# High halves of weights and feed-forward activations on ScalarE instead of GpSimd, in a two-layer hybrid mixer network

## The chip, the cores and the metric

The kernel runs on one core of a Trainium2 chip. Times are device microseconds (us) of one execution. Engines are named TensorE (PE in the profile; PEld are its weight loads), VectorE (DVE), ScalarE (ACT), GpSimd (POOL) and SyncE (SP, which only issues DMAs here). Each engine works through its own list of instructions in order; an instruction that waits holds up all that stand behind it on that engine.

## The reference, cut to what matters

A backbone of two layers runs over 256 context tokens and 256 latent tokens, 1024 wide. Each layer is a half-step gated feed-forward, four token mixers in parallel on one normalised input, and a second half-step feed-forward; all are modulated by shift, scale and gate vectors made from a conditioning vector.

```
def swiglu(h, w_up, w_down):
    a, g = jnp.split(h @ w_up, 2, axis=-1)
    return (jax.nn.silu(a) * g) @ w_down
...
def pre_norm(t, gain, m, i):
    return modulate(rms_norm(t, gain), m[..., 3 * i, :], m[..., 3 * i + 1, :])
```

The mixers are a gated delta rule, a long convolution (Hyena, by Fourier transforms), a state-space scan and a gated linear attention. Their inputs come from one projection `w_in`, their outputs go through `w_branch` and sigmoid gates into `w_out`. In the last layer only the latent tokens are needed behind the scans. All is float32.

## The kernel before, in words

**Products in three matmuls.** A float32 product is made of three matmuls in a faster, rounded format (float32r). Each operand x is split into a high half (x rounded to that format) and a low half (x minus the high half); the result is high·high + low·high + high·low. For activations the halves are called `hh`/`hl` (normalised input), `ah`/`al` (feed-forward hidden values), `yh`/`yl` (mixer outputs) and `mh`/`ml` (merged mixers). For weights they are `wh` and `wl`.

**Weights in chunks.** `wchunk` loads a chunk of 512 x 256 weights (512 KB, a tile of 128 x 1024) by a DMA from SyncE into `raw`, makes `wh` from it and then `wl` = `raw` − `wh`. There are three buffers each for `raw`, `wh` and `wl`, so a chunk's `wh` can be made once TensorE has left the chunk three before it. `dense_T_g` then issues, for each of two output tiles and four row blocks, the three matmuls of 512 columns (256 in most of layer 1 behind its mixers' start); `dense_tok_g` does the same with the weights as the moving side (lines 791 to 793).

**Feed-forward.** `ffn` goes through pairs of hidden tiles: two chunks give the `a` half, two the `g` half. ScalarE makes `sil` = silu(a) from PSUM (line 682), VectorE multiplies it by g in PSUM (line 687), then `split` makes `ah` and VectorE `al` (line 260). In the first three feed-forward stages VectorE also works through the modulation sums `aa` (lines 528 and 530), a fixed number for every two chunks: `aa` = `aw`·c + `aa` over loaded pieces of `w_ada`.

**Norms.** Before a stage, ScalarE makes `hh` (line 657), GpSimd the unrounded value `v` (line 658) and VectorE `hl` = `v` − `hh` (line 659).

**Mixers.** Two generators are woven together: the chain (gated delta rule, scans, convolutions; short steps on all engines) and the dense projections. A table of numbers sets how far each runs ahead. The engines' lists are then made by a scheduler that takes instructions by priority and its own estimate of when each is ready; `wchunk` gives its halves a higher priority than their place (`high_priority`, 240 places), except for the very first chunk.

**Who makes high halves.** Line 248: GpSimd makes `wh` and VectorE `wl` (line 249). In layer 0's mixers (`n_wp0` = 5) every fifth chunk has `wh` on ScalarE (line 245) and `wl` on GpSimd (line 246). `ah` is made by GpSimd (`i_acts` = 1, line 257), `yh` too, `mh` by ScalarE (line 255). The first feed-forward projection's first chunks have their own code (line 367), as do the few narrow columns at the start of the mixers (line 809): GpSimd.

Of the kernel before, what the change touches and what calls it, by code (L numbers as in the profile page):

```python
# [8 lines left out]
F32 = mybir.dt.float32  # L9
F32R = mybir.dt.float32r  # L10
I32 = mybir.dt.int32
AF = mybir.ActivationFunctionType
ALU = mybir.AluOpType
# [87 lines left out]
def const_inputs():  # L101
# [24 lines left out]
         "i_Td": 1, "i_W": 1, "i_bd": 0, "i_bm": 1, "i_ce": 1, "i_cz": 1, "i_gr": 1, "i_hy": 1, "i_scr": 1, "slack":  # L126
# [5 lines left out]

# [4 lines left out]
class Kern:  # L137
# [93 lines left out]
    def wchunk(self, src, nk, ncol):  # L231

        nc = self.nc
        n = nk * ncol
        r = self.raw(src.rearrange("(k p) c -> p k c", p=128), (128, nk, ncol))
        hi = self.pw.tile([128, 1024], F32R, name=self.nm("wh"), tag="wh", bufs=3)
        lo = self.pw.tile([128, 1024], F32R, name=self.nm("wl"), tag="wl", bufs=3)
        h = hi[:, :n].rearrange("p (a b) -> p a b", a=nk)
        l = lo[:, :n].rearrange("p (a b) -> p a b", a=nk)
        hold = self.nw < self.gen('n_hold', 2)  # L240
        with self.tc.issue_after(self.gate.ins) if hold else self.tc.high_priority(offset=self.gen('n_hp', 250)):
            self.nw += 1
            e = self.gen(f"n_wp{self.part}", 0)
            if e and self.nw % e == 0:
                nc.scalar.activation(h, r, AF.Copy)
                nc.gpsimd.tensor_tensor(l, r, h.bitcast(F32), op=ALU.subtract)
            else:
                nc.gpsimd.tensor_scalar(h, r, 1.0, 1.0, op0=ALU.mult, op1=ALU.mult)  # L248
                nc.vector.tensor_tensor(l, r, h.bitcast(F32), op=ALU.subtract)  # L249
        return h, l  # L250

    def split(self, x, hi, lo, eng="act"):
# [1813 lines left out]
```

## Time and profile before

| | |
|---|---|
| median of 3 runs | 2844.51 us (2844.41 to 2846.63) |
| profiled execution | 2847.14 us, its span 2845.2 us |
| granted TensorE clock, mean | 0.978 of full speed |
| busy: TensorE / its weight loads | 2689.9 us (95%) / 2289.9 us (80%) |
| busy: VectorE | 2036.7 us (72%), 3763 instructions |
| busy: GpSimd | 1038.9 us (37%), 1007 instructions |
| busy: ScalarE | 529.4 us (19%), 1044 instructions |
| DMA | 382.66 MB, 134 GB/s over the span |

The span is the time from the first to the last instruction of the profiled execution; the execution's own time has a little around it. Matmuls overlap in the records: one of 512 columns is listed with about 0.37 us, while the next starts 0.23 us later, so it is the idle time of TensorE and the granted clock that show what is lost, not the sum of the durations. A wait is put down to the instruction that ended last of those waited for.

Stages on the time axis, from the lines that run in them: start and first chunks to 71 us; first feed-forward of layer 0 to 450; mixers of layer 0 and their output projection to 1285; second feed-forward to 1690; first feed-forward of layer 1 to 2070; mixers of layer 1 to 2640; last feed-forward and output to the end.

### The profile page before, as it was taken

To read this page: it belongs to the slowest core of one execution; us is meant where nothing else is said; L and a number is where in the kernel's file an instruction comes from. 1 tells how busy PE (TensorE), PEld (TensorE's weight loads), DVE (VectorE), ACT (ScalarE), POOL (GpSimd) and SP (SyncE) were. 2 spreads that over 40 slices of the span, in tenths; PEclk is the share of its full clock that TensorE was granted. 3 is DMA by queue.
4 is the path that set the end of the run, shared out by engine and by line. 5 is a ranking of instruction groups with operands and counts; after the bars stand their busy time and mean duration, and the time that the engine had idled before them with its cause. 6 is when DMAs were issued, how large, how long until landed. Compare 5 with 4: busy or idle time off the path is not lost. (4 is left out here: it accounts for less than half of the span.)

```text
span 2845.2 us, 40232 instructions
## 1 busy us (share of the span) xinstructions
PE 2689.9 (95%) x15131; PEld 2289.9 (80%) x15131; DVE 2036.7 (72%) x3763; ACT 529.4 (19%) x1044; POOL 1038.9 (37%) x1007
## 2 busy tenths in 40 slices
PE   7999999989999999999999999999987899989998
PEld 5777767778888878877778877788877798889998
DVE  5999875699575564459965469966479877778656
ACT  2000012533224231111000020000042322311100
POOL 4333313221332554535322233322244233455443
PEclk8999999999999999999999999999999999999999
DMA  9556534322434233234644336543333344445554
GB/s 273 168 178 198 174 109 132 89 75 71 141 112 131 77 100 101 85 116 145 180 145 130 102 110 181 176 146 117 95 89 108 96 138 133 143 150 186 154 185 142
DMA packets 369697, 382.66 MB, mean 134 GB/s; under 512 B 43466, under 2 KB 317544, under 8 KB 369504
## 3 DMA queue, kind: packets, MB, share of 16 engines
q1 hardware_dynamic: 347568, 363.67, 42.7%
q10 hardware_dynamic: 21936, 16.44, 1.8%
q8 instruction: 119, 1.95, 0.3%
q14 instruction: 74, 0.61, 0.1%
HBM read 355.79 MB, written 24.25 MB: 134 GB/s over the span
## 5 line engine op out<-in xcount | busy, mean ns | idle before, releaser
L248 POOL TENSOR_SCALAR wh<-raw 128x1024 fp32r<-128x1024 f32 (+1 forms) x460 | 570.7, 1241 | 1181.7 <-PE pmm L296 716.5
L294 PE MATMUL pmm<-hh,wh 128*128 128x512 f32 (+1 forms) x2432 | 887.0, 365 | 14.8 <-ACT raw L964 8.7
L295 PE MATMUL pmm<-hh,wl 128*128 128x512 f32 (+1 forms) x2432 | 880.7, 362 | 18.8 <-DVE wl L249 18.8
L296 PE MATMUL pmm<-hl,wh 128*128 128x512 f32 (+1 forms) x2432 | 878.8, 362 | 6.3 <-DVE hl L659 6.3
L249 DVE TENSOR_TENSOR wl<-raw,wh 128x1024 fp32r<-128x1024 f32 (+1 forms) x460 | 581.8, 1266 | 388.4 <-POOL wh L248 387.7
L295 PEld LDWEIGHTS pmm<-hh,wl 128*128 128x128 f32 x2432 | 467.6, 192 | 91.1 <-DVE wl L249 26.1
L294 PEld LDWEIGHTS pmm<-hh,wh 128*128 128x128 f32 x2432 | 467.5, 192 | 86.7 <-issue 15.4
L296 PEld LDWEIGHTS pmm<-hl,wh 128*128 128x128 f32 x2432 | 467.0, 192 | 76.2 <-DVE hl L659 10.6
L530 DVE SCALAR_TENSOR_TENSOR aa<-aw,cond,aa 128x256 f32<-128x256 f32 x896 | 423.9, 534 | 0.5 <-DMA aw<-in_w_ada 0.5
L295 PE MATMUL pmm<-ah,wl 128*128 128x512 f32 (+1 forms) x704 | 256.6, 364 | 1.6 <-DVE wl L249 1.4
L294 PE MATMUL pmm<-ah,wh 128*128 128x512 f32 (+1 forms) x704 | 258.0, 366 | 0.0
L296 PE MATMUL pmm<-al,wh 128*128 128x512 f32 (+1 forms) x704 | 256.5, 364 | 0.0
L682 ACT ACTIVATE sil<-pmm 128x512 f32<-128x512 f32 (+1 forms) x88 | 48.0, 545 | 812.2 <-PE pmm L296 773.3
L257 POOL TENSOR_SCALAR ah<-sil 128x512 fp32r<-128x512 f32 (+1 forms) x88 | 71.5, 813 | 251.5 <-DVE sil L687 228.8
L295 PEld LDWEIGHTS pmm<-ah,wl 128*128 128x128 f32 x704 | 133.2, 189 | 23.9 <-DVE wl L249 3.3
L294 PEld LDWEIGHTS pmm<-ah,wh 128*128 128x128 f32 x704 | 133.3, 189 | 23.2 <-issue 2.0
L296 PEld LDWEIGHTS pmm<-al,wh 128*128 128x128 f32 x704 | 133.3, 189 | 21.5 <-issue 0.8
L793 PE MATMUL pmm<-wl,hh 128*128 128x256 f32 x416 | 120.1, 289 | 6.3 <-DVE wl L249 6.3
L791 PE MATMUL pmm<-wh,hh 128*128 128x256 f32 x416 | 120.8, 290 | 0.0
L792 PE MATMUL pmm<-wh,hl 128*128 128x256 f32 x416 | 119.6, 288 | 0.0
L260 DVE TENSOR_TENSOR al<-sil,ah 128x512 fp32r<-128x512 f32 (+1 forms) x88 | 93.0, 1057 | 18.4 <-POOL ah L257 18.4
L296 PE MATMUL pmm<-yl,wh 128*128 128x512 f32 (+1 forms) x256 | 86.5, 338 | 1.3 <-DVE yl L260 1.3
(435 smaller groups left out, 3667.3 us busy)
## 6 DMA issues: line engine op xcount, KB each, us to landing
raw<-in_ffn_up SPq DMA_DIRECT2D x172, 512.0 KB
raw<-in_w_in SPq DMA_DIRECT2D x164, 512.0 KB
aw<-in_w_ada SPq DMA_DIRECT2D x288, 256.0 KB
raw<-in_ffn_down SPq DMA_DIRECT2D x80, 512.0 KB
raw<-in_w_branch SPq DMA_DIRECT2D x32, 512.0 KB
fe<-pk SPq DMA_DIRECT2D x42, 256.0 KB
raw<-in_w_out SPq DMA_DIRECT2D x16, 512.0 KB
pk<-pj ACTq DMA_DIRECT2D x26, 256.0 KB
```

The costliest lines, as they stand in the source:

```text
L248: nc.gpsimd.tensor_scalar(h, r, 1.0, 1.0, op0=ALU.mult, op1=ALU.mult)
L249: nc.vector.tensor_tensor(l, r, h.bitcast(F32), op=ALU.subtract)
L257: nc.gpsimd.tensor_scalar(hi, x, 1.0, 1.0, op0=ALU.mult, op1=ALU.mult)
L260: nc.vector.tensor_tensor(lo, x, hi.bitcast(F32), op=ALU.subtract)
L294: nc.tensor.matmul(o, h[:, k, js], rh[:, tj:t1], start=st, stop=False)
L295: nc.tensor.matmul(o, l[:, k, js], rh[:, tj:t1], start=False, stop=False)
L296: self.last_mm = nc.tensor.matmul(o, h[:, k, js], rl[:, tj:t1], start=False, stop=sp)
L530: nc.vector.scalar_tensor_tensor(a, x, c, a, op0=ALU.mult, op1=ALU.add)
L682: self.last_act = nc.scalar.activation(s[:, t0:t1], ps, AF.Silu)
L791: nc.tensor.matmul(o, rh[:, ts], h[:, k, :], start=st, stop=False, skip_group_check=True)
L792: nc.tensor.matmul(o, rl[:, ts], h[:, k, :], start=False, stop=False, skip_group_check=True)
L793: self.last_mm = nc.tensor.matmul(o, rh[:, ts], l[:, k, :], start=False, stop=sp, skip_group_check=True)
```

## The change

In `wchunk` every chunk now takes one path: ScalarE copies `raw` into `wh` (rounding it), VectorE subtracts. The choice by `n_wp0` is gone from the code, and with it the 20 low halves that GpSimd made. `i_acts` goes from 1 to 0, so ScalarE also makes `ah`. The own code of the first projection and the narrow columns stays with GpSimd, as do `v`, `yh` and the chain's steps. Behind `wchunk` the line numbers of the changed kernel are 5 lower than before.

```diff
-        {"i_acts": 1, "n_ga01": 3, ...
+        {"i_acts": 0, "n_ga01": 3, ...
...
-            e = self.gen(f"n_wp{self.part}", 0)
-            if e and self.nw % e == 0:
-                nc.scalar.activation(h, r, AF.Copy)
-                nc.gpsimd.tensor_tensor(l, r, h.bitcast(F32), op=ALU.subtract)
-            else:
-                nc.gpsimd.tensor_scalar(h, r, 1.0, 1.0, op0=ALU.mult, op1=ALU.mult)
-                nc.vector.tensor_tensor(l, r, h.bitcast(F32), op=ALU.subtract)
+            nc.scalar.activation(h, r, AF.Copy)
+            nc.vector.tensor_tensor(l, r, h.bitcast(F32), op=ALU.subtract)
```

The scheduler makes new lists of it. In the first feed-forward stage of layer 0, GpSimd's list before has the two kinds of high halves of one pair of hidden tiles between each other:

```order
L248 TENSOR_SCALAR wh_1129<-raw_1127 128x1024
L248 TENSOR_SCALAR wh_1161<-raw_1159 128x1024
L257 TENSOR_SCALAR ah_1076<-sil_985 128x512
L248 TENSOR_SCALAR wh_1218<-raw_1216 128x1024
L257 TENSOR_SCALAR ah_1093<-sil_999 128x512
L248 TENSOR_SCALAR wh_1270<-raw_1268 128x1024
```

In the changed kernel the same six stand on ScalarE, with the `sil` of the pair between them:

```order
L677 ACTIVATE sil_985<-pmm_929 128x512
L243 ACTIVATE wh_1129<-raw_1127 128x1024
L677 ACTIVATE sil_999<-pmm_942 128x512
L243 ACTIVATE wh_1161<-raw_1159 128x1024
L250 ACTIVATE ah_1076<-sil_985 128x512
L243 ACTIVATE wh_1218<-raw_1216 128x1024
L250 ACTIVATE ah_1093<-sil_999 128x512
L243 ACTIVATE wh_1270<-raw_1268 128x1024
```

The order of the six among themselves is kept; `sil` comes first for each of the two leading `wh`.

In layer 1's mixers, in the gated delta rule, ScalarE's list before holds chain steps alone (`qkv` are convolved inputs on their way through silu, `raw_18260` the projection out of PSUM, `pj` a projection for the convolution branch):

```order
L964 ACTIVATE raw_18260<-pmm_18197 128x512
L874 ACTIVATE qkv_18259<-raw_18260,vB_14423 128x512
L964 ACTIVATE raw_18281<-pmm_18210 128x512
L874 ACTIVATE qkv_18280<-raw_18281,vB_14423 128x512
L967 ACTIVATE qkv_18259<-qkv_18259 128x512
L967 ACTIVATE qkv_18280<-qkv_18280 128x512
L1267 ACTIVATE pj_18609<-pmm_18524 128x512
```

At that place in the changed kernel three `wh` stand among them, which GpSimd had in a row before:

```order
L959 ACTIVATE raw_18260<-pmm_18197 128x512
L869 ACTIVATE qkv_18259<-raw_18260,vB_14423 128x512
L959 ACTIVATE raw_18281<-pmm_18210 128x512
L869 ACTIVATE qkv_18280<-raw_18281,vB_14423 128x512
L243 ACTIVATE wh_18649<-raw_18647 128x1024
L962 ACTIVATE qkv_18259<-qkv_18259 128x512
L962 ACTIVATE qkv_18280<-qkv_18280 128x512
L243 ACTIVATE wh_18710<-raw_18708 128x1024
L243 ACTIVATE wh_18765<-raw_18763 128x1024
L1262 ACTIVATE pj_18609<-pmm_18524 128x512
```

Two of them stand behind the `qkv` of line 962, which waits for VectorE's convolution steps.

## Rows read from the trace of the kernel before

**Rows 1.** The page: busy us, share and instructions of each engine.

```profile
PE 2689.9 (95%) x15131; PEld 2289.9 (80%) x15131; DVE 2036.7 (72%) x3763; ACT 529.4 (19%) x1044; POOL 1038.9 (37%) x1007
```

**Rows 2.** Stretches, both mixers: start:end, length; busy us (count) by engine.

```profile
450.00:1285.00 835.00, 798.66 (x4383) 676.01 (x4382) 528.45 (x1024) 248.76 (x480) 324.96 (x326) 0.99 0.34 101
...
2070.00:2640.00 570.00, 509.15 (x3615) 468.06 (x3615) 452.75 (x865) 154.10 (x329) 240.51 (x260) 0.96 0.44 131
```

**Rows 3.** TensorE's waits: whole run (first three), 71:450, 1285:1690, 1690:2070 us.

```profile
PE pmm L295 <- DVE wl L249: 20.2, 18, 3.2
...
PE pmm L296 <- DVE hl L659: 6.3, 11, 1.5
...
PE pmm L793 <- DVE wl L249: 6.3, 2, 4.2
...
PE pmm L295 <- DVE wl L249: 7.0, 5, 3.2
...
PE pmm L295 <- DVE wl L249: 5.6, 5, 2.5
...
PE pmm L295 <- DVE wl L249: 6.1, 6, 1.6
```

**Rows 4.** A stretch of the first feed-forward: PE, PEld, DVE, ACT, POOL.

```profile
142.30:284.50 142.20, 137.59 (x617) 109.89 (x616) 141.15 (x277) 5.08 (x10) 47.67 (x30) 0.99 0.62 188
```

**Rows 5.** Order of time, 126:136 us, GpSimd and VectorE: start, us, instruction.

```profile
128.03 2.50 POOL L248 TENSOR_SCALAR wh<-raw 128x1024 fp32r<-128x1024 f32 x2
...
128.10 1.52 DVE L260 TENSOR_TENSOR al<-sil,ah 128x512 fp32r<-128x512 f32 x1 [0.51 <-POOL ah L257]
...
129.55 5.21 DVE L530 SCALAR_TENSOR_TENSOR aa<-aw,cond,aa 128x256 f32<-128x256 f32 x9
...
134.68 1.21 DVE L249 TENSOR_TENSOR wl<-raw,wh 128x1024 fp32r<-128x1024 f32 x1
```

**Rows 6.** A stretch behind a `wl` wait; the clock stands behind POOL's time.

```profile
137.40:140.70 3.30, 3.30 (x9) 2.52 (x9) 3.30 (x9) 0.00 (x0) 0.00 (x0) 0.50 0.40 117
```

**Rows 7.** Groups on GpSimd the change removes: busy us, mean ns | idle.

```profile
L248 POOL TENSOR_SCALAR wh<-raw 128x1024 fp32r<-128x1024 f32 x444 | 558.3, 1258 | 1137.6 <-PE pmm L296 682.2 <-issue 206.0 <-PE pmm L792 81.3
...
L248 POOL TENSOR_SCALAR wh<-raw 128x512 fp32r<-128x512 f32 x16 | 12.4, 774 | 44.1 <-PE pmm L296 34.3 <-DMA raw<-in_ffn_down 7.1 <-issue 2.7
...
L257 POOL TENSOR_SCALAR ah<-sil 128x512 fp32r<-128x512 f32 (+1 forms) x88 | 71.5, 813 | 251.5 <-DVE sil L687 228.8
...
L246 POOL TENSOR_TENSOR wl<-raw,wh 128x1024 fp32r<-128x1024 f32 x20 | 48.4, 2421 | 83.2 <-ACT wh L245 70.7 <-issue 7.1 <-DVE X L1067 5.4
```

**Rows 8.** Groups on ScalarE of the same kind that exist already.

```profile
L245 ACT ACTIVATE wh<-raw 128x1024 fp32r<-128x1024 f32 x20 | 21.2, 1058 | 58.7 <-PE pmm L296 49.9 <-PE pmm L792 5.1 <-DMA pk<-gqk 2.2
...
L255 ACT ACTIVATE mh<-x 128x512 fp32r<-128x512 f32 x8 | 5.1, 632 | 27.1 <-POOL x L1899 27.1
```

**Rows 9.** VectorE: `aa` min/median/max ns; then groups with their means.

```profile
L530 DVE SCALAR_TENSOR_TENSOR aa<-aw,cond,aa x896: 465/473/1336, 62.0 to 1949.5; 128x256 f32<-128x256 f32 x180
...
L530 DVE SCALAR_TENSOR_TENSOR aa<-aw,cond,aa 128x256 f32<-128x256 f32 x896 | 423.9, 534 | 0.5 <-DMA aw<-in_w_ada 0.5
...
L260 DVE TENSOR_TENSOR al<-sil,ah 128x512 fp32r<-128x512 f32 x66 | 75.0, 1137 | 18.2 <-POOL ah L257 18.2
...
L687 DVE TENSOR_TENSOR sil<-sil,pmm 128x512 f32<-128x512 f32 x66 | 44.8, 679 | 8.9 <-PE pmm L296 8.8
```

**Rows 10.** The chain that ended last, dense matmuls, 256 columns: start, us.

```profile
2657.20 0.12 PE pmm L294
```

**Rows 11.** ScalarE's waits, 2070 to 2640 us: us, times, longest.

```profile
ACT gt L1883 <- PE pmm L296: 59.7, 23, 9.2
...
ACT qkv L967 <- DVE qkv L887: 22.3, 5, 15.0
```

**Rows 12.** Order of time, layer 1's gated delta rule, VectorE and ScalarE.

```profile
2196.62 6.13 DVE L887 SCALAR_TENSOR_TENSOR qkv<-raw,vB,qkv 128x508 f32<-128x508 f32 x8
...
2202.13 1.35 ACT L967 ACTIVATE qkv<-qkv 128x512 f32<-128x512 f32 x2 [14.98 <-DVE qkv L887]
```

2 rows, old and new, of the table PACE are left out of this document.

## The prediction

> **What bounds the kernel now.** I read the engine totals first: TensorE is busy for 2689.9 of 2845.2 us, and no other engine comes near [rows 1]. So the change can only be worth what TensorE stands idle, 155 us, and what it runs at half clock. By stages (the table of stretches) the idle time sits in the two mixer stages, 835.0 − 798.7 = 36 us in layer 0 and 570.0 − 509.2 = 61 us in layer 1 [rows 2]; the rest lies in the start and in the feed-forward stages. Then I asked who ended TensorE's waits. In the three feed-forward stages that run beside the modulation sums it is above all one thing: a low half `wl` that VectorE has not yet made, 7.0 + 5.6 + 6.1 = 18.7 us in 16 of the 18 waits of this kind [rows 3]. In the mixers it is many short waits for the chain of recurrent steps; `wl` accounts for 6.3 us there, at the lines where weights are the moving side [rows 3].
>
> Why is `wl` late in the feed-forward stages? VectorE is full there: 141.15 us of 142.20 in the stretch shown, while TensorE still finds time to idle [rows 4]. A `wl` stands in VectorE's queue behind a run of `aa` sums. One place shows it whole: GpSimd makes two `wh` from 128.03 on, at the same time VectorE's `al` takes 1.52 us and nine `aa` take 5.21 us, and only at 134.68 does the `wl` start for which TensorE waits [rows 5]. After such a wait TensorE's granted clock is 0.50 for some 3.3 us, its lower level of 1.2 GHz [rows 6]; I found three such stretches behind a `wl` wait in these stages.
>
> **The change part by part.** Removed from GpSimd: 570.7 us of `wh`, 71.5 us of `ah` and, in layer 0's mixers, 20 low halves of 48.4 us [rows 7]. That is 690.6 of its 1038.9 us. It costs TensorE nothing by itself, as GpSimd is idle 63% of the time; it matters through what GpSimd does to VectorE.
>
> Added to ScalarE: 444 `wh` of 1024 columns and 16 of 512, and 88 `ah`. ScalarE already makes 20 such `wh`, at 1058 ns each, and `mh` of 512 columns at 632 ns [rows 8]. So 444 × 1.058 + 16 × 0.632 + 66 × 0.632 + 22 × about 0.4 (a guess: a little over half of 632 for 256 columns) = 470 + 10 + 42 + 9 = 531 us. ScalarE goes from 529 to 1060 us, 37% of the span: it has room. A `wh` there takes as long as on an undisturbed GpSimd, so the path from landing to `wl` does not get longer by its own duration.
>
> VectorE: it gains the 20 low halves, at 1.21 us for one [rows 5] 24 us. It loses what GpSimd cost it. The `aa` have a mean of 534 ns and a median of 473 [rows 9]. `al` (both inputs in SBUF) takes 1137 ns, while the product `sil` of the same size, with one input in PSUM, takes 679 [rows 9]. The differences: 896 × 0.061 + 66 × 0.458 = 55 + 30 = 85 us, nearly all in the feed-forward stages. Upper bound of the relief there: all 85 us. Lower bound: the removed share of GpSimd's time, 690.6/1038.9 = 66%, so 56 us. I take it near the upper end, since in the feed-forward stages GpSimd does almost nothing else: 47.67 us in 30 instructions where VectorE is full [rows 4].
>
> The trace thus shows that VectorE instructions with two SBUF inputs stretch beside GpSimd and those with a PSUM input do not. The Trainium skill ("SBUF — State Buffer", Who interferes with whom) states the mechanism: a VectorE instruction with two SBUF inputs and a GpSimd instruction that reads SBUF exclude each other, the second to issue waits the first out, and ScalarE waits on no one; the 1137 against 679 ns agree. By that rule the excess goes entirely with its cause and the `wl` term below would be 18.7 instead of 16; it speaks for the top of my bounds and changes nothing else.
>
> On TensorE's path this gives three terms. (1) Feed-forward `wl` waits: with 85 us of `aa` and `al` gone VectorE is no longer full and the `wl` comes earlier; in the shown place nine `aa` of 0.473 end in 4.3 us instead of 5.21 and `al` in 0.68 instead of 1.52, 1.8 us together, and the other runs before it are quicker as well. Between 12 us (66%) and 18.7 us; I take 16. (2) The half clock behind them: three times 3.3 us at half speed are 5 us, at least 3; I take 5. (3) The starts of the feed-forward stages and mixers, where TensorE waits for `hl` (6.3 us in 11 waits [rows 3]): GpSimd makes the `v` that `hl` needs and no longer stops for `wh` in between, but ScalarE now puts a `wh` between its `hh`. Between 0 and 6.3 us; I take 4.
>
> What is late next in the feed-forward stages: `wh` stays in a queue behind `ah`, as the order shows, and `ah` waits for VectorE's product. GpSimd stood behind the same wait, so this is not new. New is that `sil` stands between them: a `wh` waits for the buffer that TensorE leaves at the end of a chunk, and the `sil` behind it is released at about the same chunk's end, so nothing is blocked for long; each `sil` may start up to 1.06 us later, and its product is wanted only two chunks on.
>
> (4) The mixers. GpSimd's chain steps (`v`, `cl`, `hf`, `x`) no longer queue behind `wh` that wait for TensorE to leave a buffer; ScalarE's do, and ScalarE has more of them: 480 instructions in layer 0's stretch against 326 on GpSimd, 329 against 260 in layer 1 [rows 2]. VectorE's short steps lose some interference. The trace of before has no such queue on ScalarE but for the 20, so I bound the term: down to −20 us (a third of layer 1's 61 us of idle time, if the chain gets quicker), up to +55 us (the slow rival below). No row decides the sign; I take 0, since the nearest row is that of the 20 `wh` that ScalarE makes already, in layer 0's mixers [rows 8], while TensorE's waits for a `wl` of line 295 number two at most in both mixers, 18 less 16 [rows 3].
>
> Sum: −16 − 5 − 4 + 0 = −25 us. The profiled execution took 2847.14 us (span 2845.2, with 1.9 us around it), which gives 2822; it lies 2.6 us over the median 2844.51, so I forecast 2844.5 − 25 = **2820 us**.
>
> **The rivals.** *ScalarE becomes the queue that chain and weights block each other in* (slower). Place: layer 1's mixers. Three `wh` buffers let a high half be made two chunks ahead; a dense chunk there is 24 matmuls of 0.12 us [rows 10], 2.9 us, so where the chain puts nothing between, the lead is 5.8 us, and less 1.06 and 1.21 for the two halves 3.5 us. ScalarE waits far longer at some chain steps: `qkv` for VectorE 22.3 us in 5 waits, the longest 15.0 [rows 11]. The order puts two `wh` right behind that `qkv`, and VectorE's eight `qkv` steps, which it waits for, take 6.13 us [rows 12]. If a dozen waits of this kind exceed the lead by 3 us each and bring a stretch of half clock (1.7 us), that is 12 × 4.7 = 55 us: 2844.5 − 25 + 55 = 2875. It decides from about six such places on, where it eats the gain. Against it: the longest group, `gt`, 59.7 us in 23 waits [rows 11], waits for TensorE's dense matmuls, and such a wait ends when the buffers of the next `wh` come free too; and the one place that I looked at closely already has its `wl` behind the same eight steps in VectorE's own queue, so there the `wh` is not late first.
>
> *The load does not matter* (no change): the idle time of the feed-forward stages stays because the same loop (product, `ah`, `wh`, `wl`) only moved to another engine, and the small gains are given back in the mixers. 2844.5 ± 5.7. The Trainium skill ("Perfetto Trace Analysis", Identifying the Most-Contended Engine) says to improve the engine with the highest load and would expect nothing from relieving one at 37%; the trace bears that out over the whole span, but not in the stretches where VectorE is the full one.
>
> *The mixers gain too* (faster still): GpSimd's chain steps come sooner and VectorE is a few per cent quicker, −20 us more: 2800.
>
> **How the numbers follow.** The forecast (2805 to 2838) 0.45, the faster rival 0.12, no change 0.16, the slower rival 0.27. A measurement of this kernel can tell about 0.2%, 5.7 us, from no change. So faster 0.57, within 0.16, slower 0.27. The range goes from 2790 (2844.5 less all of the feed-forward `wl` waits, their half clock, the `hl` waits and 20 us of the mixers, 18.7 + 5 + 6.3 + 20, with 4.5 us for what the whole-run rows leave out) to 2868 (the forecast with most of the slow rival); the forecast's own is 2805 to 2838.
>
> **What would show it.** `al` near 690 ns and `aa` near 475 in the groups of instructions; `wh` on ScalarE at 1058; no `wl` waits in the feed-forward stages and no half clock behind them; VectorE near 2037 + 24 − 85 = 1976 us in all. Wrong it is if TensorE's waits in the mixers for `wl`, or for results of ScalarE, grow by over 25 us together, or if the feed-forward `wl` waits are still there although `al` and `aa` are short.

## The result and the profile after

The changed kernel takes **2764.4 us** (median of 4 runs, 2761.2 to 2765.5); the kernel before took 2845.1 us beside it. The ratio is 0.9714, 95% interval 0.9697 to 0.9731: faster by 81 us, 2.9%. The forecast was 2820, and the time lies below the range, which ended at 2790.

The engines, first line of the page of after (before: [rows 1]): busy us, share, instructions.

```profile
PE 2660.6 (96%) x15131; PEld 2273.1 (82%) x15131; DVE 1884.6 (68%) x3783; ACT 1031.3 (37%) x1592; POOL 343.8 (12%) x439
```

ScalarE went from 529 to 1031 us (the forecast said 1060), GpSimd from 1039 to 344. VectorE fell by 152 us, although it makes 20 more low halves (24 us): a relief of 176 us, where the prediction counted 85. TensorE fell by 29 us with the same 15,131 matmuls: its stretches at a granted clock of 0.50 add up to 124 us before and 66 after, and half of the difference is 29.

Where the 81 us went is read from stages that hold the same work. The stretches are cut at the same matmuls in both traces. First before, then after; start:end, length, then busy us (count) of PE, PEld, DVE, ACT, POOL, then clock, DMA share, GB/s. Shown are the first feed-forward of layer 0, its mixers, and the mixers of layer 1 with their output projection.

```profile
71.00:458.00 387.00, 373.53 (x1679) 297.96 (x1678) 339.94 (x655) 25.93 (x47) 117.37 (x85) 0.98 0.55 165
458.00:1245.00 787.00, 752.66 (x4169) 638.07 (x4168) 505.21 (x979) 241.89 (x468) 316.70 (x316) 0.98 0.34 100
...
2023.00:2656.00 633.00, 570.01 (x3935) 518.96 (x3935) 481.65 (x924) 165.72 (x349) 259.46 (x279) 0.96 0.42 126
```

```profile
71.90:443.00 371.10, 368.71 (x1679) 296.22 (x1678) 300.33 (x653) 101.05 (x131) 0.62 (x1) 1.00 0.56 172
443.00:1218.10 775.10, 747.98 (x4169) 635.37 (x4168) 498.87 (x999) 320.15 (x549) 173.64 (x213) 0.99 0.34 102
...
1975.80:2574.20 598.40, 559.14 (x3935) 510.42 (x3934) 443.78 (x925) 283.31 (x469) 117.47 (x161) 0.97 0.45 134
```

The matmul counts agree. In the order of the program the six stages (feed-forward, mixers, feed-forward, feed-forward, mixers, feed-forward) differ in length by −15.9, −11.9, −9.8, −10.5, **−34.6** and +0.3 us. The three feed-forward stages gave 36 us and the two mixer stages 46.5; for the first the prediction had 21 (and 4 more for the starts of norms), for the second nothing. The idle time (length less TensorE's busy time) fell by 11.1, 7.2, 6.7, 7.1 and 23.7 us in the first five. VectorE's busy time fell in all five: by 39.6, 6.3 (with 24 us of new low halves in it, so by 30), 26.9, 30.5 and 37.9 us.

TensorE's waits for low halves, whole run (us, times, longest); before they are in [rows 3].

```profile
PE pmm L291 <- DVE hl L654: 3.5, 8, 0.7
...
PE pmm L788 <- DVE wl L244: 1.0, 1, 1.0
...
PE pmm L290 <- DVE wl L244: 0.8, 1, 0.8
```

20.2 and 6.3 us of `wl` waits have become 0.8 and 1.0, and `hl` went from 6.3 to 3.5. The groups that the prediction named (busy us, mean ns | idle before; before: [rows 8, 9]):

```profile
L243 ACT ACTIVATE wh<-raw 128x1024 fp32r<-128x1024 f32 x464 | 490.8, 1059 | 1054.4 <-PE pmm L291 780.8 <-issue 118.8 <-PE pmm L787 52.1
...
L525 DVE SCALAR_TENSOR_TENSOR aa<-aw,cond,aa 128x256 f32<-128x256 f32 x896 | 371.7, 481 | 0.0
...
L255 DVE TENSOR_TENSOR al<-sil,ah 128x512 fp32r<-128x512 f32 x66 | 45.4, 688 | 10.9 <-ACT ah L250 10.9
...
L682 DVE TENSOR_TENSOR sil<-sil,pmm 128x512 f32<-128x512 f32 x66 | 45.2, 684 | 12.7 <-PE pmm L291 12.6
```

`wh` on ScalarE takes 1059 ns, as foretold from the 20 that it had made before. `al` falls from 1137 to 688 and now costs what `sil` costs; `aa` falls from 534 to 481.

What happened in layer 1's mixers shows best in one place, the gated delta rule behind [rows 12]. Before, order of time, first GpSimd, then VectorE: start, us, instruction.

```profile
2191.66 1.05 POOL L248 TENSOR_SCALAR wh<-raw 128x1024 fp32r<-128x1024 f32 x1 [4.39 <-DVE P L1065]
2194.41 1.06 POOL L248 TENSOR_SCALAR wh<-raw 128x1024 fp32r<-128x1024 f32 x1 [1.71 <-PE pmm L792]
...
2191.33 0.32 DVE L1065 TENSOR_TENSOR P<-L,X 128x156 f32<-128x156 f32 x1
2191.68 1.19 DVE L1067 TENSOR_TENSOR X<-X,P 128x156 f32<-128x156 f32 x1
2192.91 0.30 DVE L1065 TENSOR_TENSOR P<-L,X 128x135 f32<-128x135 f32 x1
...
2194.32 0.25 DVE L1065 TENSOR_TENSOR P<-L,X 128x87 f32<-128x87 f32 x1 [0.15 <-DVE X L1067]
2194.60 0.97 DVE L1067 TENSOR_TENSOR X<-X,P 128x87 f32<-128x87 f32 x1
2195.49 1.21 DVE L249 TENSOR_TENSOR wl<-raw,wh 128x1024 fp32r<-128x1024 f32 x1
2196.62 6.13 DVE L887 SCALAR_TENSOR_TENSOR qkv<-raw,vB,qkv 128x508 f32<-128x508 f32 x8
...
2202.81 1.21 DVE L249 TENSOR_TENSOR wl<-raw,wh 128x1024 fp32r<-128x1024 f32 x1
```

The chain's steps `P` and `X` take turns on VectorE and get shorter as the triangle shrinks: 0.32, then 0.30. But the `X` that starts 0.02 us after a `wh` on GpSimd takes 1.19 us, and the `X` of 87 columns takes 0.97 instead of 0.25; both end 0.10 to 0.16 us after the `wh` beside them. The `wl` that follows is late, and TensorE waits 2.07 us for it at 2196.76; the next `wl` stands behind eight `qkv` steps and costs 4.18 us more at 2204.08. These two are the 6.3 us at line 793 in [rows 3]. The same steps after:

```profile
2139.64 0.32 DVE L1060 TENSOR_TENSOR P<-L,X 128x156 f32<-128x156 f32 x1
2140.00 0.32 DVE L1062 TENSOR_TENSOR X<-X,P 128x156 f32<-128x156 f32 x1
...
2141.92 0.25 DVE L1062 TENSOR_TENSOR X<-X,P 128x87 f32<-128x87 f32 x1
2142.09 1.22 DVE L244 TENSOR_TENSOR wl<-raw,wh 128x1024 fp32r<-128x1024 f32 x1
...
2144.01 4.05 DVE L882 SCALAR_TENSOR_TENSOR qkv<-raw,vB,qkv 128x510 f32<-128x510 f32 x6
...
2148.87 1.22 DVE L244 TENSOR_TENSOR wl<-raw,wh 128x1024 fp32r<-128x1024 f32 x1
```

No step shown is stretched, the first `wl` follows the `X` of 87 columns at once, and of the two waits 1.0 us is left, at line 788.

### The profile page after: what moved, and what is told of

Same layout as the page of the kernel before. It is cut to its first block, busy times and chain, and to the rows that moved or that the text cites. A ratio compares the mean times of both kernels' runs of the same rounds, so it can differ in the third digit from the quotient of the medians.

```text
span 2763.7 us, 40047 instructions
## 1 busy us (share of the span) xinstructions
PE 2660.6 (96%) x15131; PEld 2273.1 (82%) x15131; DVE 1884.6 (68%) x3783; ACT 1031.3 (37%) x1592; POOL 343.8 (12%) x439
## 4 chain that ended last, share of the span: by engine, by line
PE 63%; DVE 8%; issue 4%; ACT 3%; POOL 3%; DMA 2%; SPq 0%; ACTq 0%; DVEq 0%; POOLq 0%
PE pmm L289 17%; PE pmm L291 17%; PE pmm L290 17%; DVE wl L244 2%; PE pmm L787 1%; PE pmm L786 1%; PE pmm L788 1%; POOL v L653 1%; PE px L1099 1%; DMA fe<-pk 1%; DVE qkv L882 1%; DVE P L1060 1%; DVE X L1062 1%; ACT wh L243 1%; PE px L1807 1%
## 5 line engine op out<-in xcount | busy, mean ns | idle before, releaser
L244 DVE TENSOR_TENSOR wl<-raw,wh 128x1024 fp32r<-128x1024 f32 (+1 forms) x480 | 588.4, 1227 | 468.8 <-ACT wh L243 467.7
L243 ACT ACTIVATE wh<-raw 128x1024 fp32r<-128x1024 f32 (+1 forms) x480 | 500.8, 1044 | 1074.2 <-PE pmm L291 799.0
L525 DVE SCALAR_TENSOR_TENSOR aa<-aw,cond,aa 128x256 f32<-128x256 f32 x896 | 371.7, 481 | 0.0
L653 POOL TENSOR_SCALAR v<-u,Am,mods 128x256 f32<-128x256 f32 x72 | 56.9, 805 | 489.8 <-DVE u L627 489.8
L250 ACT ACTIVATE ah<-sil 128x512 fp32r<-128x512 f32 (+1 forms) x88 | 50.5, 574 | 122.7 <-DVE sil L682 118.3
L289 PE MATMUL pmm<-yh,wh 128*128 128x512 f32 (+1 forms) x256 | 87.7, 344 | 0.2 <-POOL yh L252 0.2
```

The source lines that it names most:

```text
L250: nc.scalar.activation(hi, x, AF.Copy)
L289: nc.tensor.matmul(o, h[:, k, js], rh[:, tj:t1], start=st, stop=False)
L525: nc.vector.scalar_tensor_tensor(a, x, c, a, op0=ALU.mult, op1=ALU.add)
L653: nc.gpsimd.tensor_scalar(v[:, sl], u[:, sl], A, B, op0=ALU.mult, op1=ALU.add)
```

## The experiments

All were timed beside the kernel before, which took 2846 us in each group. Three theories stood against each other. **A**: VectorE's steps stretch while GpSimd reads SBUF, in the mixers as in the feed-forward. **B**: GpSimd's chain steps stood in its queue behind `wh` that waited for TensorE. **C**: the path of the high half itself is better on ScalarE, and the 20 slow low halves are gone. The table gives, for the profiled executions, by how much each stage differs from before (us, cut at the same matmuls; "ffn (0,1)" is layer 0's second feed-forward). It is one execution each, up to 6 us away from the kernel's median; a stage with the same code repeats within 2 us in the feed-forward and within some 4 in the mixers.

| kernel | median us | ffn (0,0) | mixers 0 | ffn (0,1) | ffn (1,0) | mixers 1 |
|---|---|---|---|---|---|---|
| the changed kernel | 2764.4 | −15.9 | −11.9 | −9.8 | −10.5 | −34.6 |
| only the mixers' chunks | 2801.8 | +0.7 | −13.4 | +0.2 | −0.5 | −31.6 |
| only outside the mixers | 2802.3 | −17.5 | −2.7 | −9.7 | −10.5 | −5.3 |
| with a copy on GpSimd | 2840.6 | −5.6 | +6.6 | −4.4 | −3.8 | +2.3 |
| with a memset on GpSimd | 2768.8 | −15.6 | −14.8 | −10.0 | −10.3 | −31.1 |
| with half a copy | 2782.7 | −14.8 | −6.5 | −9.1 | −10.1 | −22.2 |
| with a copy in the mixers only | 2811.1 | −15.9 | +5.3 | −9.7 | −10.5 | −6.1 |
| 20 low halves to VectorE, rest as before | 2840.5 | +0.7 | −6.0 | −0.1 | −0.5 | −1.5 |
| `ah` back on GpSimd | 2763.4 | −15.4 | −14.9 | −9.8 | −10.6 | −39.0 |
| `yh` on ScalarE too | 2762.2 | −17.5 | −14.2 | −9.8 | −10.8 | −33.6 |
| `yh` and `v` on ScalarE too | 2773.6 | −15.9 | −8.2 | −12.1 | −9.2 | −30.5 |
| `ah` on GpSimd, `yh` on ScalarE | 2762.3 | −14.4 | −16.0 | −9.6 | −10.9 | −35.4 |

**The change in the mixers alone**

```diff
+            if self.part != 'f':
+                nc.scalar.activation(h, r, AF.Copy)
+                nc.vector.tensor_tensor(l, r, h.bitcast(F32), op=ALU.subtract)
-            if e and self.nw % e == 0:
+            elif e and self.nw % e == 0:
```

> The kernel before with the new path (high half on ScalarE, low half on VectorE) only for the chunks woven with the mixers' chains (layer 0 and layer 1); the feed-forward stages, their activations and the output projections stay with GpSimd. By the change's trace the mixer stages with their output projections gave 12 + 37 = 49 of the 81 us. If what they gave was made in them (any of the theories), this kernel gains 40 to 50 us: about 2798. If they only profited from what the feed-forward stages before them left (a VectorE less behind, sums done earlier), it gains under 15 us: above 2830.

2801.8 us, ratio 0.985 (0.9836 to 0.9864): 44 us faster, all of it in the two mixer stages. What the mixers gave was made in them.

**The change outside the mixers alone**: the same with `self.part == 'f'`, and `i_acts` 0.

> The complement: the new path only outside the mixers' chains (feed-forward chunks, output projections, activations); in the mixers GpSimd makes the high halves as before, with its 20 low halves. The steps of the prediction on the feed-forward stages make it 25 us faster than before, 2820; by the changed kernel's trace these stages gave about 32 us: 2813. If the two parts are independent, this gain and that of the kernel with the mixers alone add up to 81 us; if they lean on each other, their sum is at least 15 us away from 81.

2802.3 us, ratio 0.9853 (0.9838 to 0.9868): 44 us, more than the 25 and the 32 that were expected. By the table 37.7 us lie in the three feed-forward stages and 8 in the mixer stages, of which some 6 in the output projections: these stand outside the chains and so belong to this part. The two gains add up to 88 us against 81: the parts are independent within what can be told.

**GpSimd reads again, without making anything.** Each chunk's raw weights are also copied by GpSimd into the tile of the low half, which VectorE then overwrites:

```diff
             nc.scalar.activation(h, r, AF.Copy)
+            nc.gpsimd.tensor_scalar(l, r, 1.0, 1.0, op0=ALU.mult, op1=ALU.mult)
             nc.vector.tensor_tensor(l, r, h.bitcast(F32), op=ALU.subtract)
```

> The changed kernel, and besides GpSimd copies every raw chunk into the chunk's low-half tile, which VectorE then overwrites: GpSimd has its 480 steps of about 1.24 us back in its queue, waiting for TensorE to leave the same kind of buffer and reading SBUF, but ScalarE still makes the high halves. Theory A (VectorE's steps stretch when GpSimd reads SBUF): VectorE's total rises from 1885 by some 100 us and 45 to 75 of the 81 us are lost: 2810 to 2840. Theory B (GpSimd's chain steps stand behind its chunk steps): the mixers lose 40 us, the feed-forward stages little: about 2805. Theory C (the high half itself came too late from GpSimd, and the 20 slow low halves; ScalarE's path is simply better): no loss over 10 us: 2764 to 2775.

**The same queue, without reading**: `nc.gpsimd.memset(l.bitcast(F32), 0.0)`, which only writes zeros, in that place.

> The same with a memset in place of the copy: GpSimd's 480 steps of about 1.05 us stand in the same places of its queue and wait for the same buffers, but read nothing. Theory A: VectorE's durations stay as in the changed kernel, aa near 481 ns, and the time is within 12 us of it: 2764 to 2776. Theory B: as with the copy, 40 us lost in the mixers: about 2805. Theory C: no loss over 10 us. So copy minus memset is the price of GpSimd's reading, memset minus the changed kernel that of its queue (with a low half that now also waits for GpSimd).

The copy: 2840.6 us, ratio 0.9985 (0.9976 to 0.9994). The memset: 2768.8 us, ratio 0.9741 (0.9724 to 0.9758). The copy takes back nearly the whole gain, the memset 4 us of it. The views of the copy's run: engines, the copies, `aa` with its min/median/max ns, then TensorE's waits for `wl`.

```profile
PE 2687.8 (95%) x15131; PEld 2286.6 (81%) x15131; DVE 2031.9 (72%) x3783; ACT 1026.3 (36%) x1592; POOL 963.7 (34%) x919
...
L244 POOL TENSOR_SCALAR wl<-raw 128x1024 fp32r<-128x1024 f32 x464 | 601.4, 1296 | 1502.2 <-PE pmm L291 1194.5 <-PE pmm L789 119.4 <-DVE aa L526 51.5
...
L526 DVE SCALAR_TENSOR_TENSOR aa<-aw,cond,aa x896: 466/474/1284, 61.6 to 1938.7; 128x256 f32<-128x256 f32 x180
...
PE pmm L291 <- DVE wl L245: 14.1, 22, 1.4
...
PE pmm L789 <- DVE wl L245: 6.6, 2, 4.4
```

And the memset's:

```profile
PE 2653.8 (96%) x15131; PEld 2267.6 (82%) x15131; DVE 1896.2 (69%) x3783; ACT 1029.7 (37%) x1592; POOL 795.8 (29%) x919
...
L244 POOL MEMSET wl<- 128x1024 f32 x464 | 443.4, 956 | 1592.6 <-PE pmm L291 1353.9 <-PE pmm L789 108.9 <-DVE aa L526 63.4
...
L526 DVE SCALAR_TENSOR_TENSOR aa<-aw,cond,aa x896: 465/479/499, 61.3 to 1889.9; 128x256 f32<-128x256 f32 x180
...
PE pmm L291 <- DVE wl L245: 1.4, 2, 0.8
...
PE pmm L789 <- DVE wl L245: 0.9, 1, 0.9
```

Both kernels have 480 more steps than the changed one in the same places of GpSimd's queue, and in both VectorE's `wl` waits for them; VectorE's and ScalarE's instructions start in the same order in both traces, and GpSimd's too but for one pair. Only the copy stretches `aa` and the chain's steps: VectorE is busy 2031.9 against 1896.2 us, `aa` takes up to 1284 ns against 499. And only with the copy do the `wl` waits come back (14.1 + 6.6 us, two of them at the moving weights as before). Theory A holds, at 72 us; B is worth about the memset's 4 us, within the intervals nothing. C falls with the copy too, in which ScalarE makes every high half and still next to nothing is gained. One thing beside the reading differs: the copy's step is longer (1296 against 956 ns), so a `wl` could be late because it waits for the copy. The trace speaks against it: of the 24 `wl` that TensorE waits for with the copy, 22 start on VectorE without any idle time before them, and VectorE stands idle for GpSimd's step 181.0 us with the copy and 175.8 with the memset. TensorE's own waits for GpSimd in the two mixer stages are 12.9 us with the copy and 10.5 with the memset. A memset as long as the copy was not tried. In the place shown above, VectorE with the copy:

```profile
2186.47 1.04 DVE L1061 TENSOR_TENSOR P<-L,X 128x156 f32<-128x156 f32 x1
...
2189.48 1.03 DVE L1063 TENSOR_TENSOR X<-X,P 128x87 f32<-128x87 f32 x1
2190.43 1.21 DVE L245 TENSOR_TENSOR wl<-raw,wh 128x1024 fp32r<-128x1024 f32 x1
...
2192.36 4.82 DVE L883 SCALAR_TENSOR_TENSOR qkv<-raw,vB,qkv 128x510 f32<-128x510 f32 x6
...
2197.98 1.22 DVE L245 TENSOR_TENSOR wl<-raw,wh 128x1024 fp32r<-128x1024 f32 x1
```

Again a `P` of 156 columns takes 1.04 instead of 0.32, the `X` of 87 columns 1.03, and the six `qkv` 4.82 instead of 4.05. By the table, reading costs (copy less memset) 10.0 + 5.6 + 6.5 = 22 us in the feed-forward stages and 21.4 + 33.4 = 55 us in the mixers, 77 us together in these two executions, 72 between the medians.

**Half a copy**: the same on `l[:, :nk // 2]` and `r[:, :nk // 2]`, 512 columns.

> The changed kernel with GpSimd's extra copy of half of each chunk (512 of 1024 columns, some 0.65 us). Whole copies cost 2840.6 - 2768.8 = 72 us against the memset. If the loss goes with the reading time, half of it: 2769 + 36 = 2805. If VectorE has slack and only its last share counts, clearly less: below 2790; then the feed-forward stages (up to 1285 us and 1285 to 2070) lose almost nothing and the mixers the most.

2782.7 us, ratio 0.9775 (0.9755 to 0.9794): 14 us behind the memset, not 36. Its engines, copies (busy us, mean ns) and `aa`:

```profile
PE 2669.7 (96%) x15131; PEld 2283.4 (82%) x15131; DVE 1938.0 (70%) x3783; ACT 1029.2 (37%) x1592; POOL 751.2 (27%) x919
...
L244 POOL TENSOR_SCALAR wl<-raw 128x512 fp32r<-128x512 f32 (+1 forms) x480 | 407.1, 848 | 1697.1 <-PE pmm L291 1240.9 <-issue 124.3 <-PE pmm L789 107.0
...
L526 DVE SCALAR_TENSOR_TENSOR aa<-aw,cond,aa 128x256 f32<-128x256 f32 x896 | 393.7, 500 | 0.0
```

VectorE loses 42 us of busy time against 136 with whole copies, so already its stretch is under half. Of TensorE's loss the feed-forward stages have 2 us by the table, where whole copies cost 22; the mixers have 17 of 55. I read it so: in the feed-forward VectorE has room (in the first stage it is busy 300 of 371 us in the changed kernel, 311 of 372 with half copies, 334 of 381 with whole ones), and in the mixers a stretched step counts sooner.

**The whole copy in the mixers only** (the copy under `if self.part != 'f':`).

> Whole copies, but only for the chunks woven with the mixers' chains; the feed-forward stages stay as in the changed kernel. By the stages of the run with all copies the mixers lost 18 us in layer 0 and 38 in layer 1: 2764 + 56 = 2820, all of it inside these two stages. If the mixers had lost there through sums that a stretched feed-forward stage left over, under 20 us: below 2784.

2811.1 us, ratio 0.9879 (0.9859 to 0.9898): 47 us of the gain are gone, 17 in layer 0's mixers and 28.5 in layer 1's, and the feed-forward stages keep theirs to 0.1 us. This settles that the mixers lose and win by what happens in them.

**The 20 slow low halves**: the kernel before, its `nc.gpsimd.tensor_tensor(l, ...)` turned into `nc.vector.tensor_tensor(l, ...)`.

> The kernel before, with one edit: the 20 low halves that GpSimd makes in layer 0's mixers (2.42 us each, both inputs read from SBUF) are made by VectorE. If GpSimd's reading is what costs, layer 0's mixers gain: 48 of GpSimd's 325 us there, some 15% of VectorE's 52 us of stretch, 8 us, less what 20 x 1.2 = 24 us of added work on VectorE cost: net -5 to +3 us. If the lateness of these 20 was the cause of layer 0's gain, it gives 10 us or more: below 2836.

2840.5 us, ratio 0.9979 (0.9969 to 0.9988): some 6 us, all in layer 0's mixers, just beyond the expected band and short of 10. That fits 48 us less of reading that outweigh 24 us of added work on VectorE. A low half that takes 1.21 instead of 2.42 us could do it too, and this run does not separate the two. It is half as much as the whole change gave in this stage, and nothing elsewhere.

**`ah` back on GpSimd** (`i_acts` 1 in the changed kernel).

> The changed kernel, but the feed-forward activations' high halves `ah` go back to GpSimd: 88 steps, 71.5 us in the profile of before. If VectorE's steps stretch with what GpSimd reads from SBUF, the loss goes by its reading time: 71.5 of the 642 us of removed `wh` and `ah` bring about 11% of the 76 us lost with the copy (2840.6 less 2764.4): +8 us, 2773; `aa` rises by about 10 ns. If the feed-forward stages gained because the queue of `ah` and `wh` was mixed on GpSimd, nothing: 2764 within 5.

2763.4 us, ratio 0.9705 (0.9691 to 0.9720), the same as the changed kernel. My 8 us were wrong: `aa` rose by 2 ns, not 10. VectorE has 11 us more to do, and the feed-forward stages do not notice: the room that half a copy also used. With the `wh` gone from GpSimd, the part of the change that moves the activations brought nothing.

**`yh` and the narrow high halves on ScalarE too** (`split(..., "pool")` to `"act"` at two places, line 804 to `nc.scalar.activation`), **and then `v`** (line 653 to an activation with scale and bias).

> One step on from the changed kernel: the 36 `yh` and the two narrow high halves of line 804 also go from GpSimd to ScalarE, 24.5 us of reading. By the price of the copy's run (76 us for some 590 us of reading) 24.5 us are worth 3 us: 2761. If ScalarE's queue now begins to be late (it makes 36 more steps in the chains), slower: 2767 or more.

> The same, and the 88 norm steps `v` (75 us on GpSimd) on ScalarE, right behind each `hh`. By the price of reading 100 us less of it are worth 13 us; but in the norms VectorE's `hl` waits for `v`, and ScalarE makes `hh` and `v` one after the other, some 0.4 us later for each of 8 tiles in 6 norms and the start: up to 8 us back. Reading decides: 2755 to 2760; the queue decides: 2768 or more.

The first: 2762.2 us, ratio 0.9703 (0.9689 to 0.9718), not to be told from the changed kernel. The second: 2773.6 us, ratio 0.9748 (0.9734 to 0.9761): 9 us slower than the changed kernel. VectorE's `hl`, in the changed kernel and then here (idle before it, and what ended it):

```profile
L654 DVE TENSOR_TENSOR hl<-v,hh 128x512 fp32r<-128x512 f32 (+1 forms) x48 | 34.7, 723 | 10.6 <-POOL v L653 10.2
```

```profile
L654 DVE TENSOR_TENSOR hl<-v,hh 128x512 fp32r<-128x512 f32 (+1 forms) x48 | 31.8, 663 | 18.8 <-ACT v L653 18.7
```

`hl` itself is shorter, 663 against 723 ns, with `v` no longer on GpSimd; but VectorE waits 18.7 us for `v` instead of 10.2, for ScalarE makes `hh` and `v` one behind the other. By the table the loss lies in the two mixer stages, 4 us in each, which is no more than such a stage differs from one execution to the next. That the late `hl` costs the 9 us is not shown: TensorE's own waits for `hl` fell from 9.6 to 3.5 us. What grew is its waits in the two mixer stages, from 65 to 73 us, mostly for VectorE's chain steps, and its time at half clock, from 66 to 97 us. Less reading did not pay here; the cause stays open.

**`ah` on GpSimd and `yh` on ScalarE**, the two equal variants together.

> The changed kernel with `ah` back on GpSimd and `yh` and the narrow high halves on ScalarE, the two variants that were each within 3 us of it (2763.4 and 2762.2). If both small gains are real they add: 2760 or less; if the measurement cannot tell them, 2761 to 2766.

2762.3 us, ratio 0.9704 (0.9688 to 0.9721). No version was found that can be told from the changed kernel on its better side.

## Why the prediction was wrong, point by point

**The bound and the mechanism were right.** TensorE's idle time and its half clock were what there was to win, VectorE's two-SBUF steps (two inputs in SBUF, none in PSUM) stretched beside GpSimd, and the relief came from there. `al` 688 (forecast 690), `aa` 481 (475), `wh` 1059 (1058): these sizes held.

**Term (1), the `wl` waits of the feed-forward, −16 us**: 18.7 us became 0.8, so −17.9, inside the bounds. One reading in it was off: the nine `aa` do not end in 4.3 us when undisturbed, for they overlap; after the change nine in a row take 3.65 us. None of the 20 `wl` that TensorE waited for before had itself waited for its `wh`: VectorE started each without idle time, so the queue on VectorE was what made them late, as the prediction said. What the term did not hold: a wait of 6.4 us for ScalarE's `hyh` (a sine for the convolution's filter) in the first feed-forward is gone as well. It is gone also in the kernel with the copy, and still there with the change in the mixers alone, so it does not come from the reading; I take it to go with the order of the lists, which I did not try. It is one of the reasons why these stages gave 36 us.

**Term (2), the half clock, −5 us**: the granted clock was 0.50 for 13.7 + 3.4 + 3.4 = 20.5 us of these stages before and for 3.4 after; half of the 17.1 us is 8.5. I had counted three stretches of 3.3 us; the one of 6.8 us at the wait for `hyh` and one of 3.4 us in layer 1's first feed-forward were not among them.

**Term (3), the starts, −4 us**: `hl` waits fell by 2.8 us, inside the bounds.

**Term (4), the mixers, is the step that failed: "No row decides the sign; I take 0".** They gave 46.5 us, more than the feed-forward stages that the change was reckoned by, and more than twice the lower bound of −20. By the table the copy in the mixers alone takes 46 of them back, and the memset next to nothing: what the term had at 0 is GpSimd's reading beside VectorE's chain steps and low halves. The 0 goes with the sum "55 + 30 = 85 us, nearly all in the feed-forward stages", which took the two groups with the most instructions, `aa` and `al`, and in them it was right (52 + 38 = 90 us, with line 255's 22 narrow `al`). But the relief was 176 us: another 30 us came off VectorE in layer 0's mixers and 38 in layer 1's, in dozens of small groups. The rows for it were there. Two groups of VectorE before, the same step with its input in SBUF and in PSUM:

```profile
L887 DVE SCALAR_TENSOR_TENSOR qkv<-raw,vB,qkv 128x508 f32<-128x508 f32 x24 | 21.2, 903 | 0.6 <-ACT qkv L874 0.5
...
L887 DVE SCALAR_TENSOR_TENSOR qkv<-pmm,vB,qkv 128x508 f32<-128x508 f32 x16 | 11.6, 738 | 1.3 <-ACT qkv L874 1.2
```

And after:

```profile
L882 DVE SCALAR_TENSOR_TENSOR qkv<-raw,vB,qkv 128x508 f32<-128x508 f32 x24 | 17.5, 741 | 1.3 <-ACT qkv L869 1.2
...
L882 DVE SCALAR_TENSOR_TENSOR qkv<-pmm,vB,qkv 128x508 f32<-128x508 f32 x16 | 11.4, 739 | 0.0
```

903 ns against 738 before, 741 against 739 after: the comparison that I made for `al` and `sil` gives the same answer for a step of the mixers' chain, and I did not make it there. I wrote instead that VectorE's short steps "lose some interference", and took the row of 20 `wh` on ScalarE as the nearest, which says what a `wh` costs and nothing on who is stretched beside it.

How much of the mixers' gain comes through chain steps and how much through late `wl` is only read, not tried: in layer 1's stage TensorE's waits that VectorE's chain steps end fell from 30.0 to 18.8 us, those for `wl` from 7.8 to 1.0, those for low halves of activations from 5.6 to 1.5, and the stretches at half clock from 51.2 to 30.7 us. The waits that GpSimd's steps end fell too, from 7.0 to 2.0 us (5.7 with the memset): the little that theory B has.

The Trainium skill ("SBUF — State Buffer", Who interferes with whom) says that a VectorE instruction with two SBUF inputs contends with a GpSimd instruction that reads SBUF, and not with one that only writes it. The copy and the memset bear out both halves: the 248 `aa` that overlap a copy have a mean of 745 ns and the 299 that overlap a memset one of 480, against 474 and 479 for those that overlap none. The prediction cited the first half and let it raise one term, where the trace shows it in the mixers' steps as well.

**The slow rival (0.27)**, ScalarE as the queue that blocks: it did not come. ScalarE's longest waits in layer 1's mixers after (us, times, longest; before: [rows 11]):

```profile
ACT wh L243 <- PE pmm L291: 128.1, 62, 6.4
...
ACT wh L243 <- PE pmm L787: 26.9, 10, 4.3
...
ACT gt L1878 <- PE pmm L291: 7.9, 10, 2.1
```

`wh` now waits 128 us for TensorE's buffers, in 62 waits; but the chain steps behind it wait less (`gt`, the gates, 7.9 instead of 59.7 us); I take it that the `wh` ahead of them took the wait for the same matmuls over, as the argument against the rival said. TensorE's waits that ScalarE ends rose from 7.3 to 11.2 us in that stage, 4 us of the rival's 55. At the place that the rival named, `wl` comes earlier instead of later.

**No change (0.16)** had the feed-forward's idle time stay and the mixers give the rest back; neither came. It leaned on the load too: the Trainium skill ("Perfetto Trace Analysis", Identifying the Most-Contended Engine) says to take the engine with the highest occupancy as the one to optimize first. Here 2.9% came from relieving one that was busy 37% of the time, and the memset, which kept it at 29%, cost 4 us. **The mixers gain too (0.12, 2800)** was the right branch with the wrong size, and only one of its two reasons holds: VectorE is quicker, but that GpSimd's chain steps come sooner is worth little, as the memset shows.

## What to carry to other kernels

To price what GpSimd costs VectorE, go through all VectorE groups and compare each with the same shape that has an input in PSUM, or its mean with its median and minimum; sum the excess by stage, and not only in the stage where VectorE is full. In a stage of short dependent steps the stretch counts although VectorE has idle time; where VectorE has a queue of independent work, it counts, as I read the half copies, from the point at which the engine becomes full. If a step must stay on GpSimd, ask what it reads before asking how long it is busy: the memset kept GpSimd busy for 452 us and cost some 4. To tell a queue from a contention, let an engine do the same number of steps in the same places with and without reading.

## What the runs showed of the hardware that I had not expected

The loss is far from proportional to the reading: half copies, 407 us of GpSimd time against 615, cost 14 us against 72. GpSimd is held up as well. Its copies have a median of 1053 ns and a mean of 1281, half copies 620 and 848. So it was in the kernel before (`wh` of both sizes: min/median/max ns):

```profile
L248 POOL TENSOR_SCALAR wh<-raw x460: 620/1054/6787, 56.0 to 2827.9; 128x1024 fp32r<-128x1024 f32 x142, 128x512 fp32r<-128x512 f32 x12
```

The longest, from 211.43 us on, stands beside some 16 steps of VectorE that follow each other without a gap, `aa` at 0.47 us each and a `wl` of 1.21, none of them stretched. Beside the next `wh`, of 1.22 us, it is an `aa` that takes 1.26. Which of the two engines is held up thus differs from place to place, and how long GpSimd's step takes does not tell what it costs VectorE.

A step with one tensor in SBUF and a scalar per partition is stretched too, which I had not counted among those concerned: line 528, before and after (mean 400 and 351 ns; 376 with the copy, 355 with the memset). For this step the memset is not harmless either: the 22 that overlap one have a mean of 400 ns and a longest of 761, the 106 others a mean of 346.

```profile
L528 DVE TENSOR_SCALAR aa<-aw,cond 128x256 f32<-128x256 f32 x128 | 43.6, 400 | 10.5 <-PE px L535 10.2 <-DMA aw<-in_w_ada 0.3
```

```profile
L523 DVE TENSOR_SCALAR aa<-aw,cond 128x256 f32<-128x256 f32 x128 | 36.5, 351 | 19.8 <-PE px L530 19.8
```
